# Adding the modulation bias with an identity product, and copying the modulation vectors from PSUM with ACT

## Chip, core and metric

The kernel runs on one core of one Trainium2 chip. The metric is the device time of one execution in microseconds (us). Engines are named as in the profile: PE (TensorE) multiplies matrices, DVE (VectorE), ACT (ScalarE) and POOL (GpSimd) do elementwise work, SP (SyncE) starts DMAs. Every engine works through its own queue in order; all matrices here are float32 or the same bits read as float32r.

## What is computed

Four layers of a trunk (S5, retention, Hyena, S5) act on a prompt of 128 tokens and a sample of 256 tokens, each with its own conditioning vector. Every layer begins with a norm whose output is scaled and shifted by vectors made from the conditioning, and ends with a residual that a third such vector gates. The change touches only the making of these vectors:

```python
def ada_mod(cvec, w, b):
    m = (jax.nn.silu(cvec) @ w + b)[:, None, :]
    return m[..., :D_MODEL], m[..., D_MODEL:2 * D_MODEL], m[..., 2 * D_MODEL:]
...
    for i in range(DEPTH):
        sh_c, sc_c, gt_c = ada_mod(c_ctx[None, :], mod_w[i], mod_b[i])
        sh_l, sc_l, gt_l = ada_mod(c, mod_w[i], mod_b[i])
        hc = rmsnorm(xc, norm_g[i]) * (1.0 + sc_c) + sh_c
        hl = rmsnorm(xl, norm_g[i]) * (1.0 + sc_l) + sh_l
        ...
        xc = xc + gt_c * oc
        xl = xl + gt_l * ol
```

`w` of a layer is 1024 x 3072, 12.6 MB, so the four layers read 50 MB for vectors of 3072 numbers.

## The kernel before

**Modulation units.** `mod_w` of each layer is cut into 12 slabs of 1 MB. `mod_unit` (L369) loads one slab (`wr`, two buffers that the other big weights share; the first eight of layer 0 are loaded as `wm` into a pool of their own), and multiplies it by the two conditioning vectors in eight products L381 into the PSUM tile `psn`. Four slabs make a group g, and 12 groups (three a layer) exist: shift, scale and gate of each layer. The fourth slab closes the group: ACT copies the sums to `mrow` (L386), two products with the selection matrix `sel` transpose them into 16 columns of the same `psn` tile (L388; each float32 product leaves two weight loads and two matmuls in the trace), and DVE adds the bias while it writes the group's third of `mod` (L393). For the scale group (g = 1) DVE then makes `sc` (L397), and for the gate group `gt` (L402). There is one buffer of `psn`: the first L381 of the next group waits until L393 has read the last one.

**Who reads the vectors.** `adanorm` (L457) forms `hf` on ACT from `ht`, `sc` and `mod` (L476), rounds it to `hh` (L177) and takes the remainder `hl` on DVE (L178); the projections L141 multiply these. In later layers `Early` (L479) uses them before the norm is known.

**What else runs there.** While layer 0 is projected, a generator makes S5's tables: DVE multiplies (L631, L632, 128 x 512 each), adds (L636), PE multiplies and transposes (L668, L674), ACT scales (L651) and copies (L675, L677, L678), DVE finishes `Kc` (L679, L680). Six of the sixteen generator blocks also make a `CP` table that is spilled: DVE writes `CP` (L631), POOL's queue adds the second part by a DMA (L634) and stores the tile to DRAM (`scratch_cpd_dram`, L650). `CP` has one buffer there, so the next spill's L631 waits for the store of the last.

**What sets the order.** Units lie in a queue `bg`, and loops take some from it at fixed places (`tick`). But the program is built with a scheduler that simulates time and chooses the order in which instructions of all parts stand on each engine. An edit in one place can so move instructions in others.

Of the kernel before, what the change touches and what calls it, by code (L numbers as in the profile page):

```python
# [96 lines left out]
V_MODB = 0  # L97
# [10 lines left out]
def hybrid_trunk(ctx: ExitStack, tc: tile.TileContext, I, O, dbg=None, layers=(0, 1, 2, 3)):  # L108
    nc = tc.nc
    V, S, G, TE = nc.vector, nc.scalar, nc.gpsimd, nc.tensor  # L110
# [16 lines left out]
    def psn():  # L127
        return pn.tile([128, 512], F32, tag="n", name="psn")

    def load(pool, name, src, shape=None, eng=None, **kw):  # L130
        t = pool.tile(list(shape or src.shape), F32, name=name, **kw)
        (eng or nc.sync).dma_start(t, src)
        return t
# [19 lines left out]
    def weight(src):  # L153
        raw = wraw.tile(list(src.shape), F32, tag="wr", name="wr")
        nc.sync.dma_start(raw, src)
        return raw
# [180 lines left out]
    vec = load(cst, "vec", I["vec"], eng=nc.scalar)  # L337
    sel = load(cst, "sel", I["sel"], eng=nc.scalar)
    ident = load(cst, "ident", I["ident"], eng=nc.scalar)
# [29 lines left out]
    def mod_unit(i, s, pool=None):  # L369
        if pool is None:  # L370
            raw = weight(I["mod_w"][i, s])
        else:
            raw = load(pool, "wm", I["mod_w"][i, s], tag="wm")
        u, g = s % 4, s // 4
        if u == 0:
            macc[0] = psn()
        ps, macc[1] = macc[0], u == 3
        for k2 in range(2):
            for q in range(4):
                kb = q * 2 + k2  # L380
                TE.matmul(ps[q * 32:(q + 1) * 32, :256], sg[:, kb, 6 - 2 * u:38 - 2 * u], raw[:, kb, :],  # L381
                          start=u == 0 and k2 == 0, stop=u == 3 and k2 == 1)
        if u < 3:
            return
        row = tmp.tile([128, 256], F32, tag="mrow", name="mrow", bufs=1)
        S.copy(row, ps[:, :256])  # L386
        for b in range(2):
            TE.matmul(ps[:, 256 + 8 * b:264 + 8 * b], row[:, b * 128:(b + 1) * 128], sel, start=True, stop=True)  # L388
        if g == 0:
            MODS[i] = tuple(cst.tile([128, n, 2], F32, name=f"{nm}{i}") for nm, n in (("mod", 24), ("sc", NB), ("gt", NB)))  # L390
        m, sc, gt = MODS[i][:3]
        mb = vec[:, V_MODB + i * 24 + 8 * g:V_MODB + i * 24 + 8 * g + 8].rearrange("p (u b) -> p b u", b=2)
        V.tensor_add(m[:, 8 * g:8 * g + 8, :].rearrange("p (u b) r -> p b u r", b=2),  # L393
                     ps[:, 256:272].rearrange("p (b u r) -> p b u r", b=2, u=4),
                     mb.unsqueeze(3).to_broadcast([128, 2, 4, 2]))
        if g == 1:
            V.scalar_tensor_tensor(sc, m[:, 8:16, :], 1.0,  # L397
                                   vec[:, V_G + i * 8:V_G + i * 8 + 8].unsqueeze(2).to_broadcast([128, NB, 2]),
                                   op0=OP.add, op1=OP.mult)
            MODS[i] += (True,)  # L400
        if g == 2:
            V.tensor_scalar(gt, m[:, 16:24, :], GT_F[i], None, op0=OP.mult)  # L402

    def mods(i, s0, s1):
        return [lambda s=s: mod_unit(i, s) for s in range(s0, s1)]
# [965 lines left out]
    with tc.tile_pool(name="first", bufs=FB, reuse_waits="tile", side="right") as fp:  # L1371
        for s in range(8):
            mod_unit(layers[0], s, fp)
            if s == FX:
                nc.sync.dma_start(xT, I["xT"])
# [202 lines left out]
```

## Time and profile before

| What | us |
|---|---|
| median of three runs | 1635.85 |
| the three runs | 1632.05, 1635.85, 1636.39 |
| the profiled execution | 1632.28 |
| its span on the engines | 1630.5 |
| outside the span | 1.78 |

The profiled execution ran 3.57 us below the median. Its rows give, for each instruction or run of like instructions, the start, the busy time, and in brackets how long the engine had been idle and what released it. PE's clock in the rows is the mean that was granted, as a share of full speed (2.4 GHz); over the whole span it is 0.951.

### The profile page before, as it was taken

The numbers are of one execution on the slowest core, as the hardware profiler recorded it, in microseconds if no ns is written. First come the engines' busy times: TensorE is split into PE (matmuls) and PEld (weight loads), VectorE is DVE, ScalarE is ACT, GpSimd is POOL, SyncE is SP. The second block draws the span as 40 slices with busy tenths as digits, with TensorE's granted clock in tenths as the row PEclk, the third lists the DMA queues.
The fourth block names the chain that finished last, engine by engine and source line by source line (L and its number), as shares of the span: only waits on it lengthen the run. The fifth ranks groups of instructions, "written<-read, shape, count | busy, mean of one in ns | idle before, by whom it ended". The sixth has DMA issues, their size and how long they took to land. (4 is left out here: it accounts for less than half of the span.)

```text
span 1630.5 us, 27608 instructions
## 1 busy us (share of the span) xinstructions
PE 1449.2 (89%) x10370; PEld 1280.7 (79%) x10370; DVE 1246.0 (76%) x2935; ACT 692.2 (42%) x1275; POOL 664.3 (41%) x484
## 2 busy tenths in 40 slices
PE   6778787798799899999979999999999999988996
PEld 3555585577588888889968988999998898767886
DVE  8966998699886767755968887888888874379565
ACT  2434522244333333334445544546445534542443
POOL 2111242325374857551225665655666332132221
PEclk9887899899799999999989999999999999999998
DMA  9487499843555555543333322322322345577531
GB/s 359 130 260 224 150 222 253 284 178 128 216 173 179 183 207 187 183 154 130 127 125 101 101 78 75 101 84 95 100 78 94 106 174 201 167 217 196 199 130 65
DMA packets 107805, 261.39 MB, mean 160 GB/s; under 512 B 28535, under 2 KB 68568, under 8 KB 88088
## 3 DMA queue, kind: packets, MB, share of 16 engines
q1 hardware_dynamic: 80768, 200.12, 37.2%
q0 software_dynamic: 11984, 34.87, 7.7%
q10 hardware_dynamic: 14920, 24.65, 4.3%
q8 instruction: 82, 1.34, 0.3%
q14 instruction: 51, 0.42, 0.1%
HBM read 220.37 MB, written 30.83 MB: 154 GB/s over the span
## 5 line engine op out<-in xcount | busy, mean ns | idle before, releaser
L136 POOL TENSOR_TENSOR wl<-wr,wh 128x1024 fp32r<-128x1024 f32 (+2 forms) x99 | 248.9, 2515 | 300.2 <-ACT wh L164 273.6
L164 ACT CAST wh<-wr 128x1024 fp32r<-128x1024 f32 (+4 forms) x211 | 215.7, 1028 | 315.0 <-PE psd L141 200.5
L141 PE MATMUL psd<-hh,wh 128*128 128x384 f32 x880 | 307.3, 350 | 13.5 <-DVE X L798 7.0
L141 PE MATMUL psd<-hl,wh 128*128 128x384 f32 x880 | 305.7, 347 | 6.4 <-DVE hl L472 6.2
L141 PE MATMUL psd<-hh,wl 128*128 128x384 f32 x880 | 305.3, 347 | 4.7 <-POOL wl L136 2.6
L151 DVE TENSOR_TENSOR wl<-wr,wh 128x1024 fp32r<-128x1024 f32 (+3 forms) x112 | 147.2, 1315 | 71.9 <-ACT wh L164 71.5
L141 PEld LDWEIGHTS psd<-hh,wh 128*128 128x128 f32 x880 | 169.7, 193 | 26.6 <-issue 14.5
L141 PEld LDWEIGHTS psd<-hl,wh 128*128 128x128 f32 x880 | 169.9, 193 | 15.9 <-DVE hl L472 8.9
L141 PEld LDWEIGHTS psd<-hh,wl 128*128 128x128 f32 x880 | 169.7, 193 | 12.2 <-issue 5.1
L141 PE MATMUL psd<-wl,hh 128*128 128x256 f32 x384 | 110.0, 288 | 4.0 <-POOL wl L136 2.0
L141 PE MATMUL psd<-wh,hh 128*128 128x256 f32 x384 | 110.0, 292 | 2.6 <-ACT k L1077 1.6
L141 PE MATMUL psd<-wh,hl 128*128 128x256 f32 x384 | 109.0, 286 | 0.0
L381 PE MATMUL psn<-wr,sgc 128*32 128x256 f32 x640 | 58.3, 460 | 35.0 <-DMA wr<-in_mod_w_dram 23.9
L141 PE MATMUL psd<-zb,wh 128*128 128x384 f32 x240 | 80.9, 338 | 0.0
L141 PEld LDWEIGHTS psd<-wl,hh 128*128 128x128 f32 x384 | 74.1, 193 | 6.3 <-POOL wl L136 3.2
L141 PEld LDWEIGHTS psd<-wh,hh 128*128 128x128 f32 x384 | 73.3, 193 | 4.5 <-ACT k L1077 2.0
L636 POOL TENSOR_TENSOR BP<-BP,xt 128x512 f32<-128x512 f32 x32 | 47.3, 1479 | 71.9 <-DVE xt L632 36.4
L141 PEld LDWEIGHTS psd<-wh,hl 128*128 128x128 f32 x384 | 74.1, 193 | 0.1
L631 DVE TENSOR_TENSOR CP<-B,xc 128x512 f32<-128x512 f32 x52 | 52.9, 1044 | 26.5 <-DMA scratch_cpd_dram<-CP 15.6
L632 DVE TENSOR_TENSOR xt<-BI,xc 128x512 f32<-128x512 f32 x52 | 47.2, 909 | 29.6 <-POOL CP L636 17.2
L381 PEld LDWEIGHTS psn<-wr,sgc 128*32 128x32 f32 x640 | 20.0, 124 | 56.9 <-DMA wr<-in_mod_w_dram 27.8
L797 DVE TENSOR_TENSOR X<-X,m 128x64 f32<-128x64 f32 x184 | 64.2, 349 | 0.0
(385 smaller groups left out, 3843.1 us busy)
## 6 DMA issues: line engine op xcount, KB each, us to landing
wr<-in_mod_w_dram SPq DMA_DIRECT2D x40, 1024.0 KB
wr<-in_hy_w_in_dram SPq DMA_DIRECT2D x32, 1024.0 KB
wr<-in_ret_w_in_dram SPq DMA_DIRECT2D x24, 1024.0 KB
wr<-in_s_w_in_dram SPq DMA_DIRECT2D x16, 1024.0 KB
wm<-in_mod_w_dram SPq DMA_DIRECT2D x8, 1024.0 KB
CP<-xt POOLq DMA_DIRECT2D x32, 256.0 KB, 7.2
Tt<-scratch_kd_dram SPq DMA_DIRECT2D x128, 64.0 KB
wr<-in_s_w_glu_dram SPq DMA_DIRECT2D x8, 1024.0 KB
```

Source lines behind the costliest of these rows:

```text
L136: G.tensor_tensor(out, a, b, op=op)
L141: TE.matmul(out, lhs[a], rhs[b], start=start and i == 0, stop=stop and i == len(combos) - 1)
L151: V.tensor_sub(out, a, b)
L164: S.copy(hi, ap)
L381: TE.matmul(ps[q * 32:(q + 1) * 32, :256], sg[:, kb, 6 - 2 * u:38 - 2 * u], raw[:, kb, :], start=u == 0 and k2 == 0, stop=u == 3 and k2 == 1)
L631: eng.tensor_tensor(out, c1, x[:, 0].unsqueeze(2).to_broadcast([128, 4, 8, 16]), op=OP.mult)
L632: eng.tensor_tensor(t, c2, x[:, 1].unsqueeze(2).to_broadcast([128, 4, 8, 16]), op=OP.mult)
L636: add.tensor_tensor(out, out, t, op=OP.add)
L797: V.tensor_add(dst, dst, m1[:, 0])
```

## The change

The bias `mb` is now added on PE. Each of the two products with `sel` leaves its sum open (`stop=False`), and a second product adds, to the same eight columns, the identity `ident` times the bias, read from `vec` with each number repeated for the two conditioning vectors. The 16 columns in `psn` then hold the finished vectors, and ACT copies them to `mod` where DVE added before. Per group there are two more float32 products and one more ACT copy, and one DVE add less; 12 groups have 24, 12 and 12 of them. All lines behind L388 count one more in the changed kernel (`sc` at L398, the generator's multiplies at L632 and L633), save the copy, at L395.

```diff
--- before.py
+++ after.py
@@ -385,14 +385,15 @@
         row = tmp.tile([128, 256], F32, tag="mrow", name="mrow", bufs=1)
         S.copy(row, ps[:, :256])
         for b in range(2):
-            TE.matmul(ps[:, 256 + 8 * b:264 + 8 * b], row[:, b * 128:(b + 1) * 128], sel, start=True, stop=True)
+            mb = vec[:, V_MODB + i * 24 + 8 * g:V_MODB + i * 24 + 8 * g + 8].rearrange("p (u b) -> p b u", b=2)[:, b]
+            TE.matmul(ps[:, 256 + 8 * b:264 + 8 * b], row[:, b * 128:(b + 1) * 128], sel, start=True, stop=False)
+            TE.matmul(ps[:, 256 + 8 * b:264 + 8 * b].rearrange("p (u r) -> p u r", r=2), ident,
+                      mb.unsqueeze(2).to_broadcast([128, 4, 2]), start=False, stop=True)
         if g == 0:
             MODS[i] = tuple(cst.tile([128, n, 2], F32, name=f"{nm}{i}") for nm, n in (("mod", 24), ("sc", NB), ("gt", NB)))
         m, sc, gt = MODS[i][:3]
-        mb = vec[:, V_MODB + i * 24 + 8 * g:V_MODB + i * 24 + 8 * g + 8].rearrange("p (u b) -> p b u", b=2)
-        V.tensor_add(m[:, 8 * g:8 * g + 8, :].rearrange("p (u b) r -> p b u r", b=2),
-                     ps[:, 256:272].rearrange("p (b u r) -> p b u r", b=2, u=4),
-                     mb.unsqueeze(3).to_broadcast([128, 2, 4, 2]))
+        S.copy(m[:, 8 * g:8 * g + 8, :].rearrange("p (u b) r -> p b u r", b=2),
+               ps[:, 256:272].rearrange("p (b u r) -> p b u r", b=2, u=4))
         if g == 1:
             V.scalar_tensor_tensor(sc, m[:, 8:16, :], 1.0,
                                    vec[:, V_G + i * 8:V_G + i * 8 + 8].unsqueeze(2).to_broadcast([128, NB, 2]),
```

The scheduler's order changes too. First DVE at the head of layer 0, where `sc` of layer 0 is made (`ht` is the norm's product, `U` and `FI` are S5 tables). Before:

```order
L462 TENSOR_TENSOR ht<-xT,psm 128x384
L726 MEMSET U 128x8x16
L615 TENSOR_SCALAR FI<-FI,sgn 128x1024
L393 TENSOR_TENSOR mod_144<-psn,vec 128x2x4x2
L632 TENSOR_TENSOR xt<-FI,bc 128x512
L397 SCALAR_TENSOR_TENSOR sc_145<-mod_144,vec 128x16
L636 TENSOR_TENSOR BP<-BP,xt 128x512
L462 TENSOR_TENSOR ht<-xT,psm 128x384
L632 TENSOR_TENSOR xt<-FI,bc 128x512
L462 TENSOR_TENSOR ht<-xT,psm 128x384
```

After:

```order
L463 TENSOR_TENSOR ht<-xT,psm 128x384
L727 MEMSET U 128x8x16
L616 TENSOR_SCALAR FI<-FI,sgn 128x1024
L398 SCALAR_TENSOR_TENSOR sc_147<-mod_146,vec 128x16
L633 TENSOR_TENSOR xt<-FI,bc 128x512
L463 TENSOR_TENSOR ht<-xT,psm 128x384
L637 TENSOR_TENSOR BP<-BP,xt 128x512
L463 TENSOR_TENSOR ht<-xT,psm 128x384
L178 TENSOR_TENSOR hl<-hf,hh 128x384
L633 TENSOR_TENSOR xt<-FI,bc 128x512
```

`mod` is gone, and `sc` now stands directly behind the scaling of `FI`, with the generator's `xt` behind it; one `hl` also moved ahead of an `xt`.

Next ACT in layer 0, where the first group of layer 1 closes (`mrow` is the group's, `bc`, `Kc` and `PB` are the generator's, `Ss` and `X` the scan's; a row in brackets waits for the engine named). Before:

```order
L682 DMA scratch_kd_dram<-Kc 4x32x240 [waits DMAHW2_49,DVE_49,Activation_49]
L386 COPY mrow<-psn 128x256 [waits PE_49]
L751 COPY Ss<-psm 128x512 [waits PE_49]
L651 ACTIVATE bc<-bc,sgn 128x256 [waits DVE_49]
L677 COPY Kc<-psm 128x112 [waits DMAHW7_49,PE_49]
L678 COPY Kc<-psm 128x112
L761 COPY X_200<-psm 128x2x4x48 [waits PE_49] x2
```

After:

```order
L752 COPY Ss<-psm 128x512 [waits PE_49]
L386 COPY mrow<-psn 128x256 [waits PE_49]
L752 COPY Ss<-psm 128x512 [waits PE_49]
L652 ACTIVATE bc<-bc,sgn 128x256 [waits DVE_49]
L678 COPY Kc<-psm 128x112 [waits DMAHW6_49,PE_49]
L679 COPY Kc<-psm 128x112
L395 COPY mod_1994<-psn 128x2x4x2 [waits PE_49]
L762 COPY X_204<-psm 128x2x4x48 [waits PE_49] x2
```

The new copy of `mod` stands five rows behind `mrow`, behind `bc`, which waits for DVE, and two copies of `Kc`.

Last DVE ahead of the third spill of `CP` in layer 0. Before:

```order
L636 TENSOR_TENSOR BP<-BP,xt 128x512
L632 TENSOR_TENSOR xt<-BI,bc 128x512 x2
L631 TENSOR_TENSOR BP<-F_226,bc 128x512
L632 TENSOR_TENSOR xt<-FI,bc 128x512
L631 TENSOR_TENSOR CP<-B_224,bc 128x512 x2
L631 TENSOR_TENSOR BP<-F_226,bc 128x512 x2
```

After:

```order
L637 TENSOR_TENSOR BP<-BP,xt 128x512
L633 TENSOR_TENSOR xt<-BI,bc 128x512 x2
L632 TENSOR_TENSOR BP<-F_230,bc 128x512
L633 TENSOR_TENSOR xt<-FI,bc 128x512
L680 SCALAR_TENSOR_TENSOR Kc<-dmask,dsk,psm 128x16
L632 TENSOR_TENSOR BP<-F_230,bc 128x512
L637 TENSOR_TENSOR BP<-BP,xt 128x512
L681 TENSOR_TENSOR Kc<-Kc,psm 128x16
L632 TENSOR_TENSOR BP<-F_230,bc 128x512
L632 TENSOR_TENSOR CP<-B_228,bc 128x512 x2
```

Five rows (two of `Kc`, two multiplies and an add of `BP`) moved from behind the pair that writes `CP` to ahead of it.

## Rows read from the trace of the kernel before

**Rows 1.** The page: busy time of each engine, with its share and instructions
```profile
PE 1449.2 (89%) x10370; PEld 1280.7 (79%) x10370; DVE 1246.0 (76%) x2935; ACT 692.2 (42%) x1275; POOL 664.3 (41%) x484
```

**Rows 2.** Chain that ended last: start us, us, engine, tile and line
```profile
1515.03 9.21 DMA wr<-in_s_w_glu_dram
```

**Rows 3.** Line 393: count, min/median/max ns; idle ahead of it; who waited (us, times)
```profile
L393 DVE TENSOR_TENSOR mod<-psn,vec x12: 153/166/176, 33.4 to 1517.7; 128x16 f32<-128x16 f32 x12
...
  PE psn L388: 5.1, 3
...
  PE psn L381: 12.1, 4
```

**Rows 4.** Waits of PE, 0 to 480 us: total us, times, longest us
```profile
PE psn L381 <- DMA wr<-in_mod_w_dram: 21.5, 10, 4.9
...
PE psn L381 <- DMA wm<-in_mod_w_dram: 11.1, 3, 9.2
```

**Rows 5.** Timeline, 46 to 54 us: start, us, engine, line, [idle before <-releaser]
```profile
46.28 0.37 ACT L386 COPY mrow<-psn 128x256 f32<-128x256 f32 x1 [17.73 <-PE psn L381]
...
51.26 0.15 DVE L393 TENSOR_TENSOR mod<-psn,vec 128x16 f32<-128x16 f32 x1
51.37 0.69 DVE L632 TENSOR_TENSOR xt<-FI,bc 128x512 f32<-128x512 f32 x1
...
51.47 1.94 PE L381 MATMUL psn<-wr,sgc 128*32 128x256 f32 x16 [4.15 <-DVE mod L393]
...
51.98 0.17 DVE L397 SCALAR_TENSOR_TENSOR sc<-mod,vec 128x16 f32<-128x16 f32 x1
...
52.18 0.99 ACT L476 ACTIVATE hf<-ht,mod,sc 128x128 f32<-128x128 f32 x2 [5.53 <-DVE sc L397]
...
53.76 0.69 PE L141 MATMUL psd<-hh,wh 128*128 128x384 f32 x1
```

**Rows 6.** Timeline, 147 to 157 us, same columns
```profile
153.49 1.29 DVE L631 TENSOR_TENSOR CP<-B,bc 128x512 f32<-128x512 f32 x2 [6.46 <-DMA scratch_cpd_dram<-CP]
...
154.82 0.51 ACT L651 ACTIVATE bc<-bc,sgn 128x256 f32<-128x256 f32 x1 [6.90 <-DVE CP L631]
...
156.03 0.17 DVE L393 TENSOR_TENSOR mod<-psn,vec 128x16 f32<-128x16 f32 x1
...
156.25 1.08 PE L381 MATMUL psn<-wr,sgc 128*32 128x256 f32 x8 [6.60 <-DVE mod L393]
```

**Rows 7.** Timeline of PE, 209.5 to 211.3 us, same columns
```profile
210.26 0.34 PE L141 MATMUL psd<-hh,wh 128*128 128x384 f32 x1
210.44 0.51 PE L388 MATMUL psn<-sel,mrow 128*128 128x8 f32 x4
210.80 0.42 PE L141 MATMUL psd<-hl,wh 128*128 128x384 f32 x1
```

**Rows 8.** Timeline, 422 to 428 us, same columns
```profile
424.00 0.99 PE L388 MATMUL psn<-sel,mrow 128*128 128x8 f32 x4
...
426.62 0.69 PE L141 MATMUL psd<-hh,wh 128*128 128x384 f32 x1 [1.04 <-ACT wh L164]
```

**Rows 9.** Timeline, 1302 to 1308 us, same columns
```profile
1306.12 0.45 PE L141 MATMUL psd<-zhh,wh 128*128 128x384 f32 x1 [2.04 <-ACT wh L164]
```

**Rows 10.** Stretches: busy us (count) of PE, PEld, DVE, ACT, POOL; clock; DMA
```profile
147.00:157.00 10.00, 3.31 (x32) 2.21 (x36) 3.50 (x10) 3.04 (x8) 2.31 (x3) 0.56 0.60 183
205.00:216.00 11.00, 10.99 (x79) 9.80 (x81) 11.00 (x67) 2.19 (x4) 2.78 (x2) 1.00 0.78 222
245.00:257.00 12.00, 6.11 (x68) 4.01 (x69) 12.00 (x63) 1.45 (x3) 2.58 (x3) 0.88 0.96 293
368.00:378.00 10.00, 9.06 (x62) 8.16 (x63) 9.33 (x22) 2.59 (x5) 3.66 (x6) 1.00 0.54 213
```

**Rows 11.** Line 677, a small copy on ACT from PSUM, as in rows 3
```profile
L677 ACT COPY Kc<-psm x32: 229/252/312, 57.1 to 709.1; 128x112 f32<-128x112 f32 x32
```

**Rows 12.** Timeline, 135 to 137 us: the fourth of six spills
```profile
135.63 1.29 DVE L631 TENSOR_TENSOR CP<-B,bc 128x512 f32<-128x512 f32 x2 [2.54 <-DMA scratch_cpd_dram<-CP]
```

## Prediction

> **What bounds the kernel now.** I read the page's busy times first: PE is busy 89% of the span, DVE 76%, ACT 42% [rows 1]. So the change adds work to the busiest engine, takes work from the second, and gives a little to one with room. But these are averages; each of the 12 groups must be looked at where it stands. So next the view of line 393: its 12 adds cost 0.153 to 0.176 us, DVE idled 5.1 us ahead of three of them for the products L388, and PE stood 12.1 us in four places until L393 had read `psn` [rows 3]. That last figure is the largest thing the change could touch. Then the timelines around the groups, to see what else was late there, and the stretches, to see which engine had no rest. Against these waits stands another reason why PE waits at the same products L381: their slabs have not arrived, 21.5 us in ten places and 11.1 us in three [rows 4]. At the end of the program the chain goes through the load of the GLU weights, 9.21 us from 1515.03 on, past the last group [rows 2]. So most groups lie beside something longer.
>
> **Removed from DVE.** 12 adds x 0.166 = 2.0 us [rows 3]. It is worth something only where DVE has no rest and others wait for it: DVE is busy 11.00 of 11 us at 205 to 216 and 12.00 of 12 at 245 to 257 [rows 10]; there 2 x 0.166 = 0.33 us may be gained. The other ten are taken at nothing, since an engine that rests elsewhere in the stretch gives the time back as rest. I take -0.33.
>
> **The first scale vector.** In layer 0 the add stood behind the scaling of `FI` in DVE's queue, at 51.26, then an `xt` of 0.69 us, and `sc` started at 51.98; ACT had waited 5.53 us for it, and the first L141 followed at 53.76 [rows 5]. In the new order `sc` stands directly behind the scaling of `FI`, in the place where the add started. So `sc` can start up to 51.98 - 51.26 = 0.72 us earlier, some 0.07 of which I give to the overlap of neighbouring rows: 0.65 us. `hf`, `hh` and the first projection hang on it, so this is on the path. The `xt` that is overtaken starts later by the 0.17 us of `sc`, and feeds only the generator. I take -0.65.
>
> **The early read of `psn`.** The same timeline has PE idle for 4.15 us until the add [rows 5]. With the copy on ACT, which idles there after `mrow`, the wait for the add all but goes: the next slab's L381 (1.94 us) runs some 4 us earlier. But the work that PE does next is L141 at 53.76, and it waits for `hh`, so PE idles afterwards instead. What is won is only the 0.65 above.
>
> **The long wait at 156.** Here PE idled 6.60 us [rows 6], with 3.31 us of work in 10 and a granted clock of 0.56, near the lower level, 1.2 GHz [rows 10]. The reason is upstream of the add: DVE stood 6.46 us, until 153.49, for the store of the last spilled `CP` [rows 6]. The new copy doesn't get around this. It stands on ACT behind `bc`, which waited 6.90 us for that same `CP`, and behind two copies of `Kc`. After `bc` at 154.82 + 0.51 come two small copies of about 0.25 each, then the copy itself: `psn` is read at about 155.8 to 156.1, as the add does at 156.03 to 156.20. I take 0 (bounds: 0.4 gained, 0.3 lost).
>
> **The added products.** Each float32 product leaves two weight loads and two matmuls, so a group gets four more pairs. The price stands in a row of the same form: between two L141, whose starts are 0.17 us apart in that stretch, the four records of L388 sit at 210.44, and the next L141 starts at 210.80 instead of 210.43 [rows 7]. So four cost 0.37 us at the full clock; at the lower level the row is 0.99 us long [rows 8], which is the upper bound for a group. The lower bound is 0, where PE waits for something anyway. Seven groups I find covered: the two at 33 and 46 by the wait for slabs or for `sc` [rows 4, 5], the one at 156 by the spill, those near 293 and 330 by slabs [rows 4], the one at 1303 by a wait of 2.04 us for a cast behind it [rows 9], the last by the 9.21 us load [rows 2]. At 424, in spite of the lower clock, PE waits 1.04 us for a cast just behind [rows 8], which is as long as the addition; at 250 PE works 6.11 of 12 us [rows 10]. So those two are covered too. That leaves three: 82, 210 (PE busy 10.99 of 11 us) and 374 (9.06 of 10) [rows 10]: 3 x 0.37 = +1.11 us. If all 12 were exposed it would be 4.4 us, and at the lower clock 12 x 0.99 = 11.9.
>
> **The added copies.** 12 copies of 128 x 16. The nearest form on ACT is the `Kc` copy of 128 x 112 from PSUM, 0.229 to 0.312 us [rows 11], so at most 12 x 0.31 = 3.7 us, on an engine that is free 58% of the time [rows 1]. On the path I put them at 0. What can cost is not the copy but its wait: the queue behind it stands until the four products are done, and what stands there are casts of weights, `Kc` and `hf`. In the order I find the copy mostly directly behind `mrow`, whose casts behind it wait for loads or for PE in any case. In their own sentences: the Trainium skill, "PSUM — Partial Sum Buffer", on engine and sequencer instructions, says that the queues of ScalarE, VectorE and GpSimdE are strict FIFO, which speaks against a waiting copy on ACT. The trace agrees, in that `FI` and an `xt` held up `mod` and `sc` on DVE [rows 5]; but it is as true for the add on DVE as for the copy on ACT, and DVE is the fuller queue.
>
> **Reordering.** The scheduler moved five generator rows ahead of the third spill: three of 128 x 512, at 0.69 us as `xt` [rows 5], and two of 16 columns, at 0.166 as the add [rows 3], 2.4 us. The spill chain paces DVE later: the fourth spill already waits 2.54 us for the store of the third [rows 12], the fifth 6.46. A slip of 2.4 us can so come out at 156 in full; or it is absorbed, since the same five rows no longer stand behind the spill, and the generator's work as a whole is the same. Bounds 0 and +2.4 (a gain of the same size isn't excluded, as other rows moved too); I take 0, since DVE idles 9 us at these waits in any case and does the moved work in time that it would have waited.
>
> **Sum.** -0.33 - 0.65 + 1.11 = +0.1 us. 1632.28 + 0.1 = 1632.4 for an execution like the profiled one; that one was 3.57 us below the median, so 1636.0 for a median. That is no change within what a measurement of this kernel can tell, 0.3% or 4.9 us.
>
> **Rivals.**
> *PE's waits go for good* (faster). PE's 12.1 us for line 393 [rows 3] vanish, and the work behind moves up. For it: psn has one buffer, and each wait is named. Against it: at 51 PE then waits for `hh`, and at 156 the copy hangs on the same spill. If the two longest did go, 4.15 + 6.60 = 10.75 less the 0.65 counted, the time would be about 1636 - 10 = 1626. Half of it would still be faster by over 0.3%. Beside it, the Trainium skill, "TensorE: Matmul & The Clock Gate", Part 1, says that PE's clock follows how busy it has lately been. A shorter idle time at 156 would then also lift the 0.56 of that stretch; the trace agrees as to the low clock around idle stretches [rows 10], but the wait must go first.
> *The spill chain slips* (slower). One slip of 2.4 us stays within 0.3%. If it is handed on and repeated, at the fourth, fifth and sixth spill, because generator rows stand ahead of each `CP` pair and each store starts later, it is 3 x 2.4 = 7.2: 1636 + 7.2 = 1643. It decides from the second slip on. For it: the waits grow from one spill to the next, 2.54 and 6.46 [rows 6, 12]. Against: at the sixth, as at the fourth and fifth, the order differs by one to three rows only.
> *Every group's products are exposed* (slower or same). 4.4 us more at full clock, less 1.0: 1639.4, still no difference; only at the lower clock throughout, 11.9 - 1.0, is it 1647. The covers above speak against it.
> *The copy frees nothing earlier*, and the reordering has no effect: +1.1, 1637.
>
> **How the numbers follow.** No change, by the sum or by the last rival: 0.58. Faster, waits in part or whole gone, or a luckier order: 0.22. Slower, by the spills 0.14 and by the products 0.06: 0.20. The range reaches from 1628 (most of the first long wait gone, or the reordering 8 us better) to 1643 (three slips).
>
> **What would show it.** In the changed trace L381 at 51 should start near 47.5 with no wait for the copy, `sc` near 51.3 and the first L141 near 53.1. At 156 L381 should still wait over 5 us, its cause again the store of `CP`. Four added pairs at 210 should push L141 by 0.37. If the fifth spill starts later than 156, the slip is real; if L381 there starts before 152, the faster rival is. A time outside 1631 to 1641 means that the reordering, which I set at 0, was mis-sized.

## The result: slower by 0.7 to 1.1 per cent

The changed kernel took 1644.63 us (median; 1635.85 before), a ratio of 1.0072 with a 95% interval of 1.0044 to 1.0100. The ratio here and below is worked out from all runs of both kernels that were timed beside each other, save one slow run of e16 (2023.6 us, at a granted clock of 0.645); the two medians alone give 1.0054. Timed again beside other kernels (e8) the changed kernel came out at 1.0109 (1.0082 to 1.0136). The forecast was no change, 1636.0, within 1628 to 1643. So both were missed: the kernel is slower, and its median lies above the range.

Its profiled execution took 1643.49 us, with a span of 1641.7. First the page, to be set against [rows 1]:

```profile
PE 1464.2 (89%) x10418; PEld 1301.3 (79%) x10418; DVE 1250.8 (76%) x2923; ACT 694.9 (42%) x1287; POOL 659.9 (40%) x484
```

PE is busy 15.0 us longer (1464.2 against 1449.2), though only 48 pairs of records were added, 4.4 us at the 0.37 us for four of [rows 7]; the last section comes back to this. Next the copy that took the place of line 393 (columns as in [rows 3]; the line after "until" is ACT's own wait, the last two are those of the engine that waits for the copy):

```profile
L395 ACT COPY mod<-psn x12: 162/173/176, 33.6 to 1533.6; 128x16 f32<-128x16 f32 x12
...
  PE psn L390: 16.9, 10
...
  PEld psn L381: 1.1, 3
...
  PE psn L381: 0.8, 3
```

The change did what it says: PE now waits 0.8 us for the vectors where it waited 12.1 [rows 3]. But the waits of PE in the first 480 us (total us, times, longest) show what came in its place, beside [rows 4]:

```profile
PE psd L141 <- ACT wh L164: 17.9, 9, 6.7
PE psn L381 <- DMA wr<-in_mod_w_dram: 17.7, 8, 3.7
PE psm L669 <- ACT bc L652: 12.5, 2, 10.0
...
PE psn L389 <- ACT mrow L386: 5.2, 5, 3.2
...
PE psm L858 <- ACT Tm L859: 2.9, 1, 2.9
```

The same three waits in the kernel before:

```profile
PE psm L668 <- ACT bc L651: 8.5, 1, 8.5
PE psd L141 <- ACT wh L164: 7.5, 10, 2.0
...
PE psn L388 <- ACT mrow L386: 2.0, 4, 0.6
```

PE's wait for casts of weights (`wh`) is now 17.9 us, one of them 6.7 long; the wait for `bc` is 12.5 us, 10.0 in one piece; and `mrow` holds PE 5.2 us, one piece of 3.2 among them. So waits have moved: all of this view add up to 103 us, where it was 106. Which of them belong to the loss, the list doesn't tell; e1 and e2 come back to it.

### Where the time went, by stages

SP issues the weight loads in practically the same order in both kernels, so three of them serve as marks: a load of `s_w_in` near 209 us, one of `s_w_glu` near 336 and one of `ret_w_in` near 516. The timeline of SP (start us, us, queue, line), of the kernel before and then of the changed one:

```profile
209.21 0.34 SPq L155 DMA_DIRECT2D wr<-in_s_w_in_dram  x1
...
335.89 0.33 SPq L155 DMA_DIRECT2D wr<-in_s_w_glu_dram  x1
...
516.30 0.33 SPq L155 DMA_DIRECT2D wr<-in_ret_w_in_dram  x1
```

```profile
209.86 0.36 SPq L155 DMA_DIRECT2D wr<-in_s_w_in_dram  x1
...
341.44 0.33 SPq L155 DMA_DIRECT2D wr<-in_s_w_glu_dram  x1
...
526.11 0.33 SPq L155 DMA_DIRECT2D wr<-in_ret_w_in_dram  x1
```

The first mark is 0.7 us late, the second 5.6, the third 9.8, the end of the span 11.2. What was lost lies between 210 and 520 us: in layer 0's gate and GLU and in the passage to layer 1. From the third mark to the end the two take 1114.2 and 1115.6 us. The layer 0 phase with the generator, which the prediction feared for, is not late in this trace; how far such a point can be trusted, e7 and e8 show.

### The profile page after: what moved, and what is told of

The parts are those of the page before. It is cut to its first block, busy times and chain, and to the rows that moved or that the text cites. A ratio compares the mean times of both kernels' runs of the same rounds, so it can differ in the third digit from the quotient of the medians.

```text
span 1641.7 us, 27706 instructions
## 1 busy us (share of the span) xinstructions
PE 1464.2 (89%) x10418; PEld 1301.3 (79%) x10418; DVE 1250.8 (76%) x2923; ACT 694.9 (42%) x1287; POOL 659.9 (40%) x484
## 5 line engine op out<-in xcount | busy, mean ns | idle before, releaser
L164 ACT CAST wh<-wr 128x1024 fp32r<-128x1024 f32 (+4 forms) x211 | 215.9, 1029 | 344.4 <-PE psd L141 210.2
L141 PE MATMUL psd<-hh,wh 128*128 128x384 f32 x880 | 307.3, 351 | 22.3 <-ACT wh L164 9.4
L141 PE MATMUL psd<-hh,wl 128*128 128x384 f32 x880 | 306.1, 349 | 6.3 <-POOL wl L136 3.4
L141 PE MATMUL psd<-hl,wh 128*128 128x384 f32 x880 | 306.0, 348 | 4.0 <-DVE hl L473 3.8
L141 PEld LDWEIGHTS psd<-hh,wh 128*128 128x128 f32 x880 | 170.6, 194 | 34.1 <-ACT wh L164 13.5
L141 PEld LDWEIGHTS psd<-hh,wl 128*128 128x128 f32 x880 | 170.2, 193 | 13.9 <-issue 5.3
L141 PEld LDWEIGHTS psd<-hl,wh 128*128 128x128 f32 x880 | 170.2, 193 | 13.4 <-DVE hl L473 6.3
L141 PE MATMUL psd<-wl,hh 128*128 128x256 f32 x384 | 110.1, 288 | 3.9 <-POOL wl L136 2.9
L141 PE MATMUL psd<-wh,hh 128*128 128x256 f32 x384 | 110.5, 292 | 1.6 <-ACT k L1078 0.9
L141 PE MATMUL psd<-wh,hl 128*128 128x256 f32 x384 | 109.0, 286 | 0.0
L141 PE MATMUL psd<-zb,wh 128*128 128x384 f32 x240 | 81.1, 338 | 0.0
L141 PEld LDWEIGHTS psd<-wl,hh 128*128 128x128 f32 x384 | 74.2, 193 | 5.8 <-POOL wl L136 3.9
L381 PE MATMUL psn<-wr,sgc 128*32 128x256 f32 x640 | 56.7, 437 | 21.6 <-DMA wr<-in_mod_w_dram 21.0
L141 PEld LDWEIGHTS psd<-wh,hh 128*128 128x128 f32 x384 | 73.5, 193 | 2.9 <-DVE g L535 1.2
L141 PEld LDWEIGHTS psd<-wh,hl 128*128 128x128 f32 x384 | 74.0, 193 | 0.1
L633 DVE TENSOR_TENSOR xt<-BI,xc 128x512 f32<-128x512 f32 x52 | 47.2, 910 | 29.7 <-POOL CP L637 16.7
L632 DVE TENSOR_TENSOR CP<-B,xc 128x512 f32<-128x512 f32 x52 | 51.8, 1026 | 22.8 <-DMA scratch_cpd_dram<-CP 9.7
L635 POOL DMA_DIRECT2D CP<-xt x32 | 27.9, 915 | 91.6 <-DVE xt L633 37.0
```

What stands on the lines that cost most here:

```text
L141: TE.matmul(out, lhs[a], rhs[b], start=start and i == 0, stop=stop and i == len(combos) - 1)
L164: S.copy(hi, ap)
L632: eng.tensor_tensor(out, c1, x[:, 0].unsqueeze(2).to_broadcast([128, 4, 8, 16]), op=OP.mult)
L633: eng.tensor_tensor(t, c2, x[:, 1].unsqueeze(2).to_broadcast([128, 4, 8, 16]), op=OP.mult)
L635: nc.gpsimd.dma_start(out, t, accum_op=OP.add)
```

## Experiments

Two theories were set against each other. **A, order:** the edit made the scheduler choose another order for hundreds of other instructions, and that order is worse. **B, work:** the added products and copies cost the time.

The instrument is a kernel whose order is held. It is traced twice; the first program gives the order of each engine, and the second gets an edge, without a wait, from each instruction to the one that stands behind it in that order. Only the instructions of the edit itself (identity products, and the copy or the add) are left free:

```diff
+def pin(tc, traced, order):
+    nosync = mybir.DependencyInfo(mybir.DependencyClass.NoSync, mybir.DependencyReason.DATA)
+    for e, ks in order.items():
+        t = traced[e]
...
+        for a, b in zip(ks, ks[1:]):
+            tc.add_manual_dep(t[b], t[a].name, nosync, reason="pin")
...
+    for CH[0] in TURNS:
```

With `TURNS` as (0, 1) it is the change in the old order, with (1, 0) the old code in the new. Holding an order costs nothing that shows: e12 below, the old code held in the old order, came out at 0.9994, and e11 and e13, the change held in the new order, at 1.0089 and 1.0084, between the two timings of the changed kernel (each has one further small edit).

### e1 and e15: the change in the old order

> The whole change, but every other instruction is held, on each engine, in the order that it has in the kernel before; only the identity products, the copies on ACT and the missing adds differ. Theory A (the loss of 8.8 us comes from the order that the scheduler chose anew): within 3 us of the kernel before, 1633 to 1639. Theory B (the loss comes from the added products and copies themselves): 1642 to 1648, as the changed kernel. Something between, near 1640, would mean that both carry about half.

> The first run again (the change held in the old order), for a narrower interval: 1.000 to 1.005 in the first run. If order is most of the loss, 1.001 to 1.004 again; a value above 1.006 would say that the change's own work is most of it after all.

Measured: 1.0024 (0.9999 to 1.0048), and again 1.0038 (1.0023 to 1.0054). So with the old order kept the change costs 0.2 to 0.4%, some 4 to 6 us, less than half of what it costs with the scheduler free.

### e2 and e16: the old code in the new order

> The kernel before, with the bias added on DVE and no identity product, but every other instruction held in the order that it has in the changed kernel. Theory A (order): 1642 to 1648, though none of the change's work is done. Theory B (work): 1633 to 1639.

> The second run again (the old code held in the new order), for a narrower interval: 1.005 to 1.008 in the second run. If order is most of the loss, 1.005 to 1.009 again; a value below 1.003 would say that the order alone does little.

Measured: 1.0067 (1.0051 to 1.0084), and again 1.0043 (1.0021 to 1.0065). None of the change's work is done here, and yet 0.4 to 0.7% is lost. The repeat fell just under the band that it was given. A holds for the larger part, B for a smaller one; the two means, 0.31% and 0.55%, add up to 0.86%, against 0.72% and 1.09% for the changed kernel.

The waits of the result part in the same way. In the new order PE waits long for `bc` and `mrow` even with the old code (12.5 and 5.2 us in e2, 11.2 and 5.4 in e16), and in the old order for less, without the change (8.5 and 2.0 before, 5.2 and 2.0 in its second trace, e7) and with it (3.4 and 2.0 in e1, 3.9 and 2.0 in e15). So these two go with the order. The long wait for `wh` is no mark of it: it is 17.3 and 16.8 us in e1 and e15, which lose less than half a per cent.

### e3 and e4: a third and a fourth order

e3 puts DVE back for the copy, with the products kept; e4 keeps the copy on ACT and leaves the bias out:

```diff
 e3
-        S.copy(m[:, 8 * g:8 * g + 8, :]...
+        V.tensor_copy(m[:, 8 * g:8 * g + 8, :]...
 e4
-        V.tensor_add(m[:, 8 * g:8 * g + 8, :]...
+        S.copy(m[:, 8 * g:8 * g + 8, :]...
```

> The identity products as in the change, but DVE copies the finished vectors from PSUM where ACT does in the change; the scheduler is free. Theory B (work): if the products cost the time, 1642 to 1648; if the copies on ACT do, 1633 to 1639. Theory A (order): any of these, since this kernel gets a third order of its own; a time outside both bands would speak for A.

> ACT copies the vectors from PSUM as in the change, but the bias is left out altogether (no identity product, no add), so less is done than in either kernel; the scheduler is free. Theory B (work): with the products gone 1633 to 1639 if they cost the time, 1642 to 1648 if the copies on ACT do. Theory A (order): again an order of its own, and it may be slower than the kernel before in spite of having less work.

Measured: e3 1.0083 (1.0066 to 1.0100), e4 1.0097 (1.0082 to 1.0112). By B alone one of them had to be near 1, or each between, if products and copies cost half each; both are as slow as the change or slower. e4 does less work than the kernel before and is no faster than the change.

### e10: the copies alone, in the old order

This has just the instructions of e4, but in the order of the kernel before.

> The copies on ACT alone, held in the old order: no identity product, and the bias is left out. If the products carry what the change's work costs (1.0024), this is 1.000; if the copies do, 1.0024 again. The intervals are as wide as that difference, so the trace decides: from 335 to 510 us the first run fell back by 2.7 us against the kernel before, a second trace of which fell back by 1.2. Products: at most 1.2 here. Copies: 2.5 or more.

Measured: 1.0008 (0.9984 to 1.0032). The same instructions cost 0.97% in one order and 0.08% in the other. That is the plainest proof of A: nothing differs but the order (and the edges that hold it). And the copies on ACT are free within what can be measured, some 4 us either way. By the expectation the trace was to decide, and it does not fall back from 335 to 510 us either (179.4 us from mark 2 to 3 in the table below, where e1 takes 183.1), so what the change's work costs is carried by the products.

### e9: five products for one, in the old order

```diff
-            if CH[0]: SPECIAL.append(TE.matmul(..., ident, ..., start=False, stop=True))
+            for n in range(5 * CH[0]): SPECIAL.append(TE.matmul(..., ident, ..., start=False, stop=n == 4))
```

> The change held in the old order, as in the first run, but with five identity products for each one of the change (the bias is so added five times): eight more products in each of the 12 groups. By the price read from the rows, 0.37 us for two products at full clock, that is 1.48 us a group. If three groups are exposed, as predicted, 4.4 us over the first run's 1.0024, so near 1.005; if all are, 17.8 us, near 1.013; if PE's clock is low at all of them, up to 48 us, near 1.03.

Measured: 1.0106 (1.0072 to 1.0139). Over the mean of e1 and e15 (1.0031) that is 0.75%, 12.2 us for 96 more products, 0.13 us each. By the two intervals it may be 0.07 to 0.19 us each. For the change's own 24 products that makes 3.1 us (1.6 to 4.5), more than the 1.11 forecast. How many groups pay it doesn't tell: at the full clock a fully exposed product costs 0.37 / 2 = 0.185 us [rows 7], and 0.13 would be some 8 groups of 12; at the lower clock it costs up to 0.99 / 2 [rows 8], and three groups would do.

### e5 and e6: which part of the order

The order is spliced: up to the instruction that closes the second group of layer 1 it is taken from one program, behind it from the other.

> The change with the order of the kernel before on every engine until the second group of layer 1 is closed (about 215 us), and the new order from there on. If the loss of 8 to 9 us comes from the order behind 215 us, as the traces of single executions suggest (0.7 us late at 215, 11 us late at 560), this is as slow as the changed kernel: 1642 to 1648. If it comes from the generator's order in layer 0, 1634 to 1639.

> The change with the new order until the second group of layer 1 is closed (about 215 us), and the order of the kernel before from there on. The opposite of the last run: 1634 to 1639 if the order behind 215 us costs the time, 1642 to 1648 if the order of layer 0's generator does. If both this and the last come out near 1640, the loss is spread over both parts.

Measured: e5 1.0071 (1.0046 to 1.0096), e6 1.0052 (1.0031 to 1.0074). Both lose, the later part of the order more; the intervals overlap, so the split is not settled by the times. By the stages below e6 takes about as long as the change in the old order from its first mark on; e5 takes as long as the change in the new one from mark 2 to 3, and lies between the two from mark 1 to 2.

### e7 and e8: second traces

> The kernel before, once more, for a second trace: the same median within 0.3%. Where its trace stands against the first one tells how much of a difference of two single traces is chance: if single traces agree within 1 us at 200, 560 and 1300 us, the steps seen in the changed kernel's trace are its own; if they differ by several us, a step in one trace proves nothing.

> The changed kernel once more, for a second trace: the ratio 1.007 again, within its interval. The steps that belong to its order come again in the second trace (0.7 us late at 215, 4 at 265, 5.6 at 320, 8 at 410, 11 at 510); those that don't were chance.

Measured: e7 1.0002 (0.9978 to 1.0027), e8 1.0109 (1.0082 to 1.0136). Single executions scatter: e7 reached the first mark 5.1 us ahead of the first trace of the same kernel, so a difference of two traces at one point proves nothing. Nor do ratios from two timings tell small differences: that of the changed kernel moved from 1.0072 to 1.0109. But the lengths of the two middle stages come again, within 1.3 us for two traces of a kernel. In us, worked out from SP's rows as above (to the first mark, first to second, second to third, third to the end):

| Kernel | to mark 1 | 1 to 2 | 2 to 3 | to the end | ratio |
|---|---|---|---|---|---|
| before, two traces | 209.2, 204.1 | 126.7, 127.0 | 180.4, 181.7 | 1114.2, 1116.2 | 1 |
| e12: old code, old order, stores on POOL | 210.2 | 128.3 | 183.5 | 1111.3 | 0.9994 |
| e10: copies, old order | 212.2 | 126.6 | 179.4 | 1115.8 | 1.0008 |
| e1, e15: change, old order | 213.5, 212.7 | 126.8, 127.4 | 183.1, 183.2 | 1114.9, 1114.3 | 1.0024, 1.0038 |
| e6: new order, then old | 215.1 | 126.8 | 182.0 | 1116.3 | 1.0052 |
| e2, e16: old code, new order | 211.6, 208.0 | 127.7, 128.2 | 184.1, 183.9 | 1116.0, 1110.6 | 1.0067, 1.0043 |
| e5: old order, then new | 212.1 | 129.8 | 184.3 | 1116.5 | 1.0071 |
| change, two traces | 209.9, 213.2 | 131.6, 132.3 | 184.7, 184.1 | 1115.6, 1118.1 | 1.0072, 1.0109 |
| e9: five products, old order | 215.9 | 132.4 | 185.2 | 1122.3 | 1.0106 |
| e3: products, copies on DVE, free order | 216.3 | 121.4 | 185.0 | 1120.7 | 1.0083 |
| e4: copies, free order | 211.7 | 138.8 | 184.1 | 1113.3 | 1.0097 |

The rows of e15 and e2 for it, as examples:

```profile
212.67 0.33 SPq L155 DMA_DIRECT2D wr<-in_s_w_in_dram  x1
...
340.08 0.33 SPq L155 DMA_DIRECT2D wr<-in_s_w_glu_dram  x1
...
523.25 0.33 SPq L155 DMA_DIRECT2D wr<-in_ret_w_in_dram  x1
```

```profile
211.57 0.35 SPq L155 DMA_DIRECT2D wr<-in_s_w_in_dram  x1
...
339.25 0.33 SPq L155 DMA_DIRECT2D wr<-in_s_w_glu_dram  x1
...
523.31 0.33 SPq L155 DMA_DIRECT2D wr<-in_ret_w_in_dram  x1
```

From mark 2 to 3 the old code in the new order loses 3 us, the change in the old order 2, and both together 3.5. From mark 1 to 2 the work alone costs nothing, the new order alone 1 us, and both together 5; five products for one in the old order (e9) lose 5 there too. The first stage scatters by 5 us between two traces of one kernel and the last by up to 5.4 (e2 and e16), too much to read a cause from; only e9 and e3 lie above all others from mark 3 on (e3 has an order of its own, in which one load of `mod_w` has another place between the first two marks). And e12, described next, takes 1.5 and 2.5 us more than the kernel before (mean of its two traces) in the two middle stages and is no slower in all. So a step of 2 us in one trace is at the limit of what this table can show.

### e11 and e12: a stall of ACT, taken away

In the changed kernel's trace ACT stands some 12 us, until 265, ahead of a store of the scan's states, and PE then waits 2.9 us for the copies (`Tm`) behind it, the last row of the waits above:

```profile
265.10 0.56 ACTq L800 DMA_DIRECT2D out_ns_dram<-XF  x1
265.75 1.07 ACT L859 COPY Tm<-psm 128x512 f32<-128x512 f32 x2 [12.43 <-DVE X L798]
```

What held the store no view names. Its data, `XF`, were written by 258.7, and that it waits for a load to land, as the next expectation has it, is not shown. e11 (new order, the change) and e12 (old order, old code) let POOL issue these stores:

```diff
-            nc.scalar.dma_start(O["ns5"][j]...
+            nc.gpsimd.dma_start(O["ns5"][j]...
```

> The change in its new order, but the stores of the scan's final states are issued by POOL and not by ACT; all else is held in place. In the changed kernel ACT stood 12 us ahead of such a store at 265 us (it waits for an earlier load to land), and PE waited 2.9 us for the copies behind it. If that stall is a part of the loss, the step of 3 us at 260 us goes and the ratio falls by about 0.002, to 1.006 or 1.007. If the stall only covers another wait, the step stays and the ratio is 1.007 to 1.011.

> The kernel before, in its own order, with the same stores issued by POOL. Its ACT stood 11.75 us there as well, but PE waited only 0.2 us for it. So nothing is to be won here by removing the stall as such: ratio 0.998 to 1.002. If it is faster than 0.998, it beats both kernels, and the stall cost the old order too.

Measured: e11 1.0089 (1.0055 to 1.0124), e12 0.9994 (0.9972 to 1.0015). From mark 1 to 2 e11 takes 132.2 us, as the changed kernel does (131.6, 132.3). So that stall, plain as it stood in the trace, was only a cover for something else that is as late, and my reading of it as a cause is wrong. Counted from mark 1, PE starts the products behind `Tm` at 53.9 us in e11 and not at 56.5, but the next of them wait as long as the first did before, for nothing that the profile names, and start at 57.9, where it was 58.2. PE's waits from 255 to 290 us in e11 (total us, times, longest):

```profile
PE psm L857 <- issue: 2.9, 1, 2.9
```

e12 is no faster than the kernel before either.

### e13 and e14: one swapped pair, both ways

Near 430 us the traces of the new order show a wait that those of the old lack. On ACT, the cast of a retention weight (L164) stands ahead of `mrow`. The changed kernel (start us, us, engine, line, idle before and releaser), and behind it e15 in the old order:

```profile
432.44 1.04 ACT L164 CAST wh<-wr 128x1024 fp32r<-128x1024 f32 x1 [10.75 <-DMA scratch_line_dram<-ex]
...
433.40 0.36 ACT L386 COPY mrow<-psn 128x256 f32<-128x256 f32 x1
...
433.81 0.60 PE L389 MATMUL psn<-sel,mrow 128*128 128x8 f32 x2 [3.24 <-ACT mrow L386]
```

```profile
429.49 0.37 ACT L386 COPY mrow<-psn 128x256 f32<-128x256 f32 x1 [8.55 <-PE psn L381]
...
429.91 0.39 PE L389 MATMUL psn<-sel,mrow 128*128 128x8 f32 x2
...
432.35 1.99 ACT L164 CAST wh<-wr 128x1024 fp32r<-128x1024 f32 x2 [0.71 <-DMA wr<-in_ret_w_in_dram]
```

In the first, `mrow` stands until the cast has had its turn, which a DMA allows only at 432.44 (the row names a store; in e14's, below, it is the load of the cast's weight), and PE waits 3.24 us for `mrow`; in the second `mrow` is there at 429.49 and PE goes on. e13 undoes this one swap in the new order, e14 makes it in the old (the expectation calls the group a scale group, which it can't be: the last `sc` of the changed kernel starts at 393.7 us):

```diff
 e13, new order
+            p = ks.index(t.index(MROW[9]))
+            ks[p - 1], ks[p] = ks[p], ks[p - 1]
 e14, old order
+            p = ks.index(t.index(MROW[9]))
+            ks.insert(p, ks.pop(p + 4))
```

> The change in its new order with one swap undone: on ACT, the copy of the sums of the scale group of the fourth layer (mrow, near 430 us) stands ahead of the cast of a retention weight again, as in the old order, and not behind it. In the changed kernel that cast waited for its load, and PE 2.4 to 3.2 us for the copy behind it. If this swap makes the step of 2.7 us between 420 and 460 us, PE's wait for mrow goes there and that step falls below 1 us; the ratio falls by about 0.0015, to 1.007 or 1.008. If the wait only covers another (the load, or the next layer's first projections), the step stays.

> The opposite: the change in the old order, with that one cast put ahead of mrow on ACT. If the swap makes the step, PE waits 2 to 3 us for mrow near 430 us and falls back by 2 to 3 us between 420 and 460 us, and the ratio is 1.004. If not, the trace is as that of the first run, 0.4 us at most.

Measured: e14 1.0043 (1.0025 to 1.0062), e13 1.0084 (1.0055 to 1.0112). The trace of e14 has the wait, longer still:

```profile
430.03 1.04 ACT L164 CAST wh<-wr 128x1024 fp32r<-128x1024 f32 x1 [12.60 <-DMA wr<-in_ret_w_in_dram]
...
430.98 0.37 ACT L386 COPY mrow<-psn 128x256 f32<-128x256 f32 x1
...
431.40 0.59 PE L389 MATMUL psn<-sel,mrow 128*128 128x8 f32 x2 [5.41 <-ACT mrow L386]
```

and its stage from mark 2 to 3 is 185.0 us against 183.1 and 183.2 without the swap: made alone, the swap lengthens this stage by 2 us. In the total it isn't shown, since 1.0043 lies within the intervals of e1 and e15. And undone alone it gains nothing: e13's stage is 184.2 us, as before the repair (184.7, 184.1). Its rows, and one of PE's waits from 405 to 470 us:

```profile
431.67 0.37 ACT L386 COPY mrow<-psn 128x256 f32<-128x256 f32 x1 [8.58 <-PE psn L381]
...
432.10 0.39 PE L389 MATMUL psn<-sel,mrow 128*128 128x8 f32 x2
...
433.16 1.99 ACT L164 CAST wh<-wr 128x1024 fp32r<-128x1024 f32 x2 [1.12 <-DMA wr<-in_ret_w_in_dram]
```

```profile
PE psd L141 <- ACT hh L471: 3.2, 1, 3.2
```

The wait for `mrow` is gone, and PE waits 3.2 us for `hh` at the same place instead, which the casts now hold up. At this place, as at `Tm`, the new order has several things late at once; mending one uncovers the next.

## Why the prediction was wrong

**Reordering, "I take 0" with bounds of 0 and 2.4 us: the step that failed.** I priced one moved group of rows (the third spill) and took the rest as a permutation that would cancel. By e2 and e16 the order alone costs 0.43 to 0.67%, 7 to 11 us, and by e10 against e4, whose order is another one again, 14.5 us for the same instructions. The prediction's own sign for it, a time outside 1631 to 1641, has come. The rival on the spill chain had the right sign and nearly the right time (1643), but by chance, with the wrong mechanism: the slip was not handed on. The third and the fourth spill do start later, by 4.9 and 3.0 us (119.77 and 138.58, before 114.91 and 135.63), but the fifth starts earlier than before, at 149.21, having waited 0.26 us in place of 6.46, and the sixth at the same time (177.54 and 177.60):

```profile
149.21 1.29 DVE L632 TENSOR_TENSOR CP<-B,bc 128x512 f32<-128x512 f32 x2 [0.26 <-DMA scratch_cpd_dram<-CP]
...
151.90 0.17 ACT L395 COPY mod<-psn 128x16 f32<-128x16 f32 x1 [0.56 <-PE psn L390]
...
153.44 1.93 PE L381 MATMUL psn<-wr,sgc 128*32 128x256 f32 x16
...
160.23 1.94 PE L381 MATMUL psn<-wr,sgc 128*32 128x256 f32 x16 [3.25 <-DMA wr<-in_mod_w_dram]
```

So the long wait at 156 [rows 6] did go, against the prediction ("L381 should still wait over 5 us"), and won nothing: the next slab at 160.23 waits 3.25 us for its load, and the products behind the next `bc`, for which PE waits 10.0 us (the row of the waits above), start at 179.42, where they started at 179.47 before. First the changed kernel's row, then that of the kernel before:

```profile
179.42 1.08 PE L669 MATMUL psm<-BP,bc 128*32 128x128 f32 x16 [10.01 <-ACT bc L652]
...
179.47 1.08 PE L668 MATMUL psm<-BP,bc 128*32 128x128 f32 x16 [8.49 <-ACT bc L651]
```

**The added products, 1.11 us: mis-sized too.** The price at the full clock was nearly right: at 210 the next L141 now starts 0.98 us behind the last, where it was 0.54 [rows 7], 0.44 us for two products against 0.37:

```profile
211.00 0.34 PE L141 MATMUL psd<-hh,wh 128*128 128x384 f32 x1
211.17 0.28 PE L389 MATMUL psn<-sel,mrow 128*128 128x8 f32 x2
211.31 0.37 PE L390 MATMUL psn<-vec,ident 128*128 128x8 f32 x2
211.54 0.37 PE L389 MATMUL psn<-sel,mrow 128*128 128x8 f32 x2
211.76 0.37 PE L390 MATMUL psn<-vec,ident 128*128 128x8 f32 x2
211.98 0.42 PE L141 MATMUL psd<-hl,wh 128*128 128x384 f32 x1
```

But not every group runs at that clock. In the one that closes at 151, where the granted clock is 0.66 of full speed from 147 to 157, nearer its lower level, the rows of L389 and L390 stand 0.43 to 0.50 us apart (149.98, 150.43, 150.86, 151.29), and 0.14 to 0.23 here. And I took nine groups as covered because a wait stood near them. e9 puts the change's products at 3.1 us, and e1 and e15 give 4 to 6 for its whole work; which of the two, price or count, was further off stays open. A wait close by covers an added product only if what ends the wait doesn't itself hang on that product; no run tests that group by group.

**The added copies, 0: right, within what can be measured.** e10 gives 1.0008 (0.9984 to 1.0032) with all twelve.

**The first scale vector, -0.65: right in place.** `sc` starts at 51.43 (51.3 was forecast) and the first L141 at 53.20 (53.1), 0.56 us earlier than before [rows 5]:

```profile
48.22 0.37 ACT L386 COPY mrow<-psn 128x256 f32<-128x256 f32 x1 [14.49 <-PE psn L381]
...
49.74 0.17 ACT L395 COPY mod<-psn 128x16 f32<-128x16 f32 x1 [1.15 <-PE psn L390]
...
49.97 1.07 PE L381 MATMUL psn<-wr,sgc 128*32 128x256 f32 x16 [0.26 <-ACT mod L395]
...
51.43 0.15 DVE L398 SCALAR_TENSOR_TENSOR sc<-mod,vec 128x16 f32<-128x16 f32 x1
...
53.20 0.62 PE L141 MATMUL psd<-hh,wh 128*128 128x384 f32 x2 [2.16 <-ACT hh L177]
```

The next slab's L381 began at 49.97 and waited 0.26 us; the forecast of 47.5 was off because `mrow` itself came 1.9 us later. Whether the gain lasts isn't shown: at the first mark the kernel is 0.7 us late in this trace, and two traces of one kernel differ by 5.1 us there.

**PE's waits for line 393** went as the first rival said, 12.1 us down to 0.8, and the time rose. Of the 12.1 a part was chance: in the second trace of the kernel before (e7) they are 7.3. What stood against that rival (something else is late next) was right.

## What to carry over

In a program whose order a scheduler chooses, an edit of a few small instructions is also a new draw of the order of all others, and in a kernel whose order had come out well (all three free orders here, those of the change, e3 and e4, are slower) that draw may cost more than the edit: here 7 to 11 us against 4 to 6 for its work. Before such an edit is judged, hold the order and measure it in both; the same 24 products and 12 copies are worth 0.3% so, and 0.7 to 1.1% with the order set free. And a wait that stands out in a trace is a cause only when taking it away moves the stage's length: of the three that were removed here (the wait for the add, ACT's store, the cast ahead of `mrow`), none shortened its stage.

## What was not expected of the hardware, and what stays open

Single executions of one kernel scatter by more than the effect of many edits: the kernel before ran between 1621.5 and 1644.1 us over all its timings, and its two traces are 5.1 us apart at 210 us already. In the two stages behind that point two traces of a kernel agree to 1.3 us, so these lengths tell more than one execution's total; in the long last stage they differ by up to 5.4.

Not settled: why the new order and the products together lose 5 us from mark 1 to mark 2, where either alone loses 0 to 1; how much of the loss lies in the first 210 us; and which moved instructions make up the new order's 3 us from mark 2 to 3. The cast ahead of `mrow` may be one: made in the old order it lengthens that stage by 2 us, undone in the new order it gains nothing.

Nor is it settled what part PE's clock has in the loss. In the two traces of the changed kernel PE isn't idle for longer than in those of the kernel before (span less busy time: 177.5 and 180.6 us, before 181.3 and 175.3), but busy for 10 to 18 us longer (1464.2 and 1467.1, before 1449.2 and 1453.7). The granted clock is lower, 0.90 in both from mark 2 to 3, where it was 0.93 in both. With the old code in the new order (e2, e16) it is the other way round: PE is no busier (1451.2, 1446.3) but idle for longer (188.1, 184.4). No run holds the clock, so whether it makes a part of the loss or only follows the waits isn't shown.
